# Operand places of the 256-column products, both softmax shares of a head together, and one conditioning half behind the recurrent mixer

## Chip, cores and metric

The kernel runs on one core of one Trainium2 chip. The metric is the device time of one execution in microseconds (us). Every time below is of that one core. The engines are TensorE (PE in the profile, its weight loads PEld), VectorE (DVE), ScalarE (ACT), GpSimd (POOL) and SyncE (SP), which issues most of the DMAs.

## The reference, cut to what matters

A block of two layers over 512 tokens of width 1024, all in fp32. Layer 0 has a gated recurrent mixer (HGRN2), layer 1 a dilated attention of three groups; each is followed by a SwiGLU feed-forward network (FFN). Shift, scale and gate of each half layer come from a conditioning vector `c`.

```python
cond = jax.nn.silu(c)
for layer in range(DEPTH):                                   # 2
    mod = (cond @ ada_w[layer] + ada_b[layer])[:, None, :]   # [1024] x [1024, 6144]
    sh1, sc1, g1, sh2, sc2, g2 = jnp.split(mod, 6, axis=-1)
    u = rms_norm(h, norm_g[layer, 0]) * (1.0 + sc1) + sh1
    y = hgrn2_mixer(u, ...) if layer == 0 else dilated_attention_mixer(u, ...)
    h = h + (1.0 + g1) * rms_norm(y, norm_g[layer, 1])
    u = rms_norm(h, norm_g[layer, 2]) * (1.0 + sc2) + sh2
    gate, up = jnp.split(u @ ffn_w_in, 2, axis=-1)           # [512,1024] x [1024,5632]
    y = (jax.nn.silu(gate) * up) @ ffn_w_out
    h = h + (1.0 + g2) * rms_norm(y, norm_g[layer, 3])
```

In the attention, each group makes an output and a log-sum-exp per token and head; the outputs are weighted by a softmax over the groups:

```python
wts = jax.nn.softmax(jnp.stack(lses, axis=0), axis=0)
o = jnp.einsum('gbsh,gbshd->bshd', wts, jnp.stack(outs, axis=0))
return o.reshape(B, S, D_MODEL) @ w_out
```

## The kernel before, in words

**Products.** An fp32 operand is split into a high and a low part (`hi`, `lo` of weights; `uh`, `ul` of activations, each held as 128 partitions x 8 blocks x 512 tokens), and a product of a 128-row block is three PE passes: high by high, low by high, high by low (L577 to L579 in the helper for the plain products). Most products stream 512 columns. Some are made on 256-column halves:

- `mixer_out` (L699), the mixer's output projection of either layer, streams the halves of tokens for its last blocks, which lets the norm and residual of one half start sooner (L577 to L579 too, 336 products of 128x256 in all).
- `seven_products` (L882), most filters of the FFN's input projection: a filter is 128 gate and 128 up columns, and its 2 x 2 blocks of weights and of tokens are multiplied by seven block products in place of eight, from sums of weight blocks and of token blocks. A filter is seven calls of `run` (L958), of 4 x 3 = 12 products each, 84 in all, at L964. The sums of tokens (`th`, `tl`) are made once ahead (L864 to L879); those of weights per filter by POOL (L935) and DVE (L939, L943), split by ACT (L927, L951) and DVE (L931, L955). The first filters of each FFN (`PLAIN`: three pairs of 256 columns in layer 0, two in layer 1) are made as plain 512-column products. So FFN 0 has 16 filters by sevens and FFN 1 has 18.
- In the attention, queries and keys of two groups and the values (`products`, L1976, issued at L1982) are made by the same kind of seven products on 256 columns.

**Places.** A split weight goes to one of the buffers `hi` or `lo`, 128 x (2048 + 128) elements; `places(i, first)` (L117) lets it begin at column `first` of that buffer, so the stationary operand's byte address can be shifted. The constants R0 = 16 and V0 = 32 (L36) are the columns for the FFN's and the queries' and keys' parts, and for the values' parts. `mixer_out`'s pieces (`Stream.pieces`, L97) begin at column 0. In `seven_products` the first of the seven runs uses the token block B11. For filter 0 it is read where it lies in `uh` and `ul`; `shift()` (L893 to L897) then copies it to 144 columns further on, and all later filters read that copy:

```python
B11 = [u_of(0, 0), [(uh[:, k, 144:400], ul[:, k, 144:400]) for k in range(4)]]
```

**Order of the work.** All 1 MB weight loads, also those of the conditioning matrix `ada_w`, go through one list `items` (L485 and on) and two raw buffers: SP issues the load of an item when a raw buffer is free, and the items are worked off in the order of the list. A weight item costs ACT one cast (L89) and DVE one subtraction (L90); an `ada` item costs DVE four multiply-adds over 128 x 512 (L390, L392), and after the second of a half POOL's `partition_all_reduce` (L394); a `fin` item turns a finished half into columns with four diagonal sums (L404) and small operations (L408, L410). `hg_o` are the four pieces of the recurrent mixer's output weights, `f0a` the loads of FFN 0's input weights (six plain ones, then the filters of the sevens), `shift` the items of the conditioning vector (1, 4), that is layer 1's scale ahead of its FFN: two halves of two loads and one `fin` each. In the stage where the recurrent mixer ends, DVE, PE and POOL follow the order of the program: POOL's power `orr` (L592) gives the inverse root of the head norm, DVE multiplies by it (`aT`, L1589), PE transposes the result (L1596).

**Softmax of groups.** Per head, group 0 (natural token order, N) has its maximum and sum in `sN`, groups 1 and 2 (dilated order, R) in `sR`; each is sent to DRAM and read back in the other order (`oR`, `oN`; POOL issues these DMAs, L2261 and L2282 to L2290). `shares(own, other)` (L2293) works out one side's share with eight small DVE operations and one exponential on ACT; `merged(hd)` (L2309) calls it for R, scales the R probabilities on ACT (L2314), then for N, and scales those (L2319). A planner with costs orders these tasks among the products.

## Time and profile before

| | us |
|---|---|
| median of 3 runs (lowest, highest) | 1510.85 (1510.26, 1512.8) |
| the profiled execution | 1511.48 |
| its span in the trace | 1509.5 |
| PE busy | 1481.1 (98%) |
| DVE busy | 1108.2 (73%) |
| ACT busy | 799.6 (53%) |
| POOL busy | 200.7 (13%) |
| mean granted clock of PE | 0.995 |

The span leaves out 2 us around the program, which are part of the execution's time. A row of the timeline reads: start, duration, engine, line, operation, output<-inputs, shape, count, and in brackets the idle time of the engine just before with what ended it. A matmul's duration overlaps the next one's, so the pace of products is read from the distance of their starts, or from a window's length divided by its products. A row of the windows reads: bounds, sum of busy time, PE's busy time with the count of its instructions, granted clock (1.00 is full), the DMA engines' share, GB/s. A row of the waits reads: engine, what waited, what it waited for, total us, times, longest.

### The profile page before, as it was taken

The page shows a single profiled execution, that of the slowest core. Times are in us where ns is not written, and L with a number is a line of the kernel's source. Part 1 is how long each engine was busy: PE and PEld are TensorE (multiplying, and loading weights), DVE is VectorE, ACT ScalarE, POOL GpSimd, SP SyncE. Part 2 cuts the span into 40 slices and gives each one's busy share as a digit, 9 for nine tenths or more (in the row PEclk, how much of TensorE's full clock was granted, in tenths as well). Part 3 has the DMA queues.
Part 4 walks back from the last instruction along what each step waited for, and adds up shares of the span by engine and source line. Part 5 has one row for each costly group of instructions (what it writes and reads, how often), then busy time and mean ns, then how long its engine had stood idle before and what let it go on. Part 6 is the DMA issues. An engine that isn't in the chain of part 4 may idle for free. (4 is left out here: it accounts for less than half of the span.)

```text
span 1509.5 us, 25145 instructions
## 1 busy us (share of the span) xinstructions
PE 1481.1 (98%) x9807; PEld 1324.4 (88%) x9807; DVE 1108.2 (73%) x1896; ACT 799.6 (53%) x1482; POOL 200.7 (13%) x174
## 2 busy tenths in 40 slices
PE   8999999899999999999999999999999999999998
PEld 6777888788999997888998989999988899999886
DVE  4577768478688876777798777888776978887533
ACT  4443433273455542357647777557886555555231
POOL 1011211131111111131001010001012211110100
PEclk9999999999999999999999999999999999999999
DMA  9553445215233346634344343344343333334531
GB/s 308 165 185 126 154 154 195 84 57 180 86 112 109 115 136 223 225 110 150 105 134 127 105 110 85 108 138 134 92 154 126 100 97 113 113 112 140 195 112 56
DMA packets 210151, 201.09 MB, mean 133 GB/s; under 512 B 8248, under 2 KB 167920, under 8 KB 209776
## 3 DMA queue, kind: packets, MB, share of 16 engines
q1 hardware_dynamic: 207056, 192.71, 40.8%
q10 hardware_dynamic: 1952, 6.65, 1.2%
q8 instruction: 77, 1.26, 0.4%
q0 software_dynamic: 1024, 0.13, 0.2%
q14 instruction: 42, 0.34, 0.1%
HBM read 192.31 MB, written 5.31 MB: 131 GB/s over the span
## 5 line engine op out<-in xcount | busy, mean ns | idle before, releaser
L89 ACT CAST hi<-raw 128x2048 fp32r<-128x2048 f32 x43 | 82.1, 1910 | 135.8 <-DMA raw<-in_ffn_w_out_dram 69.4
L577 PE MATMUL ps_mm<-uh,hi 128*128 128x512 f32 (+1 forms) x400 | 146.3, 366 | 0.0
L578 PE MATMUL ps_mm<-ul,hi 128*128 128x512 f32 (+1 forms) x400 | 144.3, 361 | 1.0 <-DVE ul L677 1.0
L579 PE MATMUL ps_mm<-uh,lo 128*128 128x512 f32 (+1 forms) x400 | 144.6, 361 | 0.0
L1982 PE MATMUL ps_mm<-apart,hiq 128*128 128x256 f32 (+1 forms) x608 | 142.5, 327 | 0.0
L90 DVE TENSOR_TENSOR lo<-raw,hi 128x2048 fp32r<-128x2048 f32 x43 | 101.0, 2352 | 56.3 <-ACT hi L89 56.3
L1982 PEld LDWEIGHTS ps_mm<-apart,hiq 128*128 128x128 f32 x608 | 99.8, 188 | 8.1
L1982 PE MATMUL ps_mm<-apart,loq 128*128 128x256 f32 (+1 forms) x304 | 97.7, 321 | 0.0
L964 PE MATMUL ps_mm<-th,hiq 128*128 128x256 f32 x340 | 93.9, 276 | 0.0
L964 PE MATMUL ps_mm<-tl,hiq 128*128 128x256 f32 x340 | 93.9, 276 | 0.0
L964 PE MATMUL ps_mm<-th,loq 128*128 128x256 f32 x340 | 93.9, 276 | 0.0
L955 DVE TENSOR_TENSOR loq<-raw,hiq 128x1024 fp32r<-128x1024 f32 x68 | 80.2, 1220 | 18.5 <-ACT hiq L951 18.5
L577 PEld LDWEIGHTS ps_mm<-uh,hi 128*128 128x128 f32 x400 | 75.5, 189 | 19.7 <-issue 8.4
L578 PEld LDWEIGHTS ps_mm<-ul,hi 128*128 128x128 f32 x400 | 75.6, 189 | 12.0 <-DVE ul L677 1.4
L579 PEld LDWEIGHTS ps_mm<-uh,lo 128*128 128x128 f32 x400 | 75.5, 189 | 11.5
L935 POOL TENSOR_TENSOR raw<-raw 128x512 f32<-128x512 f32 x34 | 44.7, 1315 | 302.7 <-DVE spare L931 138.2
L577 PE MATMUL ps_mm<-hi,oh 128*128 128x512 f32 x208 | 82.1, 395 | 0.7 <-ACT hi L89 0.7
L578 PE MATMUL ps_mm<-lo,oh 128*128 128x512 f32 x208 | 81.7, 393 | 0.4 <-DVE lo L90 0.4
L951 ACT CAST hiq<-raw 128x1024 fp32r<-128x1024 f32 x68 | 68.0, 1046 | 18.4 <-DVE raw L939 17.5
L1982 PE MATMUL ps_mm<-uh,hiq 128*128 128x256 f32 x256 | 72.6, 283 | 3.4 <-ACT ps_mm L2071 2.9
L1982 PE MATMUL ps_mm<-uh,loq 128*128 128x256 f32 x256 | 71.7, 280 | 0.1
L1982 PE MATMUL ps_mm<-ul,hiq 128*128 128x256 f32 x256 | 71.6, 280 | 0.0
(486 smaller groups left out, 4659.6 us busy)
## 6 DMA issues: line engine op xcount, KB each, us to landing
raw<-in_ada_w_dram SPq DMA_DIRECT2D x40, 1024.0 KB, 5.2
raw<-in_ffn_w_in_dram SPq DMA_DIRECT2D x136, 256.0 KB, 3.7
raw<-in_ffn_w_out_dram SPq DMA_DIRECT2D x22, 1024.0 KB, 5.1
raw<-in_attn_w_in_dram SPq DMA_DIRECT2D x64, 256.0 KB, 4.7
raw<-in_hgrn_w_in_dram SPq DMA_DIRECT2D x12, 1024.0 KB, 5.3
raw<-in_attn_w_in_dram SPq DMA_DIRECT2D x12, 1024.0 KB, 5.0
raw<-in_ffn_w_in_dram SPq DMA_DIRECT2D x10, 1024.0 KB, 5.2
raw<-in_attn_w_in_dram SPq DMA_DIRECT2D x16, 512.0 KB, 5.2
```

Of the source, the lines that this page charges most:

```text
L89: self.nc.scalar.copy(hi, t)
L90: self.nc.vector.tensor_sub(lo, t, hi.bitcast(F32))
L577: pe.matmul(ps, ah, bh, start=start, stop=False, skip_group_check=part)
L578: pe.matmul(ps, ah, bl, start=False, stop=False, skip_group_check=part)
L579: pe.matmul(ps, al, bh, start=False, stop=stop, skip_group_check=part)
L935: pool.tensor_add(r[:, 2], r[:, 2], r[:, 0])
L951: act.copy(hi, src)
L955: dve.tensor_sub(lo, src, hi.bitcast(F32))
L964: pe.matmul(ps, w[x][:, a], us[kt][y], start=begin and kt + m == 0, stop=kt == 3 and m == 2, skip_group_check=True)
L1982: pe.matmul(dst(), x, y, start=begin and i == 0, stop=i == len(todo) - 1, skip_group_check=True)
```

## The change

Three things are changed.

**Places.** The first two `pieces` calls of `mixer_out` begin at column 16. The queries' and keys' parts take a column per head (`Q0`), the values' parts one per unit (`V0`). `shift()` and the copy are gone: every filter's first run reads B11 in its own place. All 256-column products of `mixer_out` and of the FFN then have a distance of 64 between the stationary and the moving operand's byte address, modulo 512.

```diff
-R0, V0 = 16, 32
+R0, V0, Q0 = 16, (112, 96, 64, 16), (16, 16, 16, 16, 48, 80, 112, 0)
...
-            (hi_a, lo_a), (hi_b, lo_b) = st.pieces(2)
+            (hi_a, lo_a), (hi_b, lo_b) = st.pieces(2, first=R0)
...
-            B11 = [u_of(0, 0), [(uh[:, k, 144:400], ul[:, k, 144:400]) for k in range(4)]]
-
-            def shift():
-
-                for a, b in ((112, 256), (0, 112)):
-                    for copy, t in ((act.copy, uh), (dve.tensor_copy, ul)):
-                        copy(t[:, 0:4, a + 144:b + 144], t[:, 0:4, a:b].bitcast(F32))
+            B11 = u_of(0, 0)
...
-                    run(s.first, R, 0, B11[i > 0], True)
+                    run(s.first, R, 0, B11, True)
...
-                    if i == 0:
-                        shift()
...
-                s_["p1"] = split_place(R0)
+                s_["p1"] = split_place(Q0[hd])
...
-                    ps[0] = split_place(V0)
+                    ps[0] = split_place(V0[i * 2 + hf])
```

**Shares.** One tile `so` (128 x 2 x 2 x 4 x 2: own or other, R or N, token tile, maximum or sum) takes the place of `sN`, `sR`, `oN` and `oR`. `merged` works out both shares in one go: six small DVE operations and one exponential per head instead of sixteen and two. The R probabilities' scaling now comes behind both read-backs.

```diff
+            reads = [so("R"), so("oR"), so("oN")] + [so(n, t) for n in "RN" for t in range(NT)]
+            DVE(0.2, lambda: dve.tensor_tensor(M.t, so.t[:, 0, :, :, 0], so.t[:, 1, :, :, 0], op=OP.max), reads, [M()])
+            DVE(0.2, lambda: dve.tensor_sub(e.t, so.t[:, :, :, :, 0], M.t.unsqueeze(1).broadcast_to((P, 2, 2, NT))), reads + [M()], [e()])
+            ACT(0.22, lambda: act.activation(e.t, e.t, AF.Exp), w=[e()])
+            DVE(0.2, lambda: dve.tensor_mul(z.t, e.t, so.t[:, :, :, :, 1]), reads + [e()], [z()])
+            DVE(0.2, lambda: dve.tensor_add(z.t[:, 0], z.t[:, 0], z.t[:, 1]), w=[z()])
+            DVE(0.22, lambda: dve.reciprocal(z.t[:, 0], z.t[:, 0]), w=[z()])
+            DVE(0.2, lambda: dve.tensor_mul(e.t[:, 0], e.t[:, 0], z.t[:, 0]), [z()], [e()])
```

**Order of items.** The second load of the conditioning vector's half 1 and that half's `fin` move from among `hg_o` into FFN 0's plain loads; half 0's `fin` comes earlier.

```diff
-        items += weave(hg_o, shift[1:4], 0)
+        items += [hg_o[0], *shift[1], hg_o[1], shift[3][0], hg_o[2], *shift[2], hg_o[3]]
...
-        items += weave(f0a[:n0], shift[5:] + gate_loads[:2] + [gate_fins[:1]], 2) + f0a[n0:]
+        items += weave(f0a[:n0], [shift[3][1:], shift[5] + gate_loads[0], gate_loads[1], gate_fins[:1]], 2) + f0a[n0:]
```

SP's loads from the mixer's last output weights to the end of FFN 0's plain loads, in the kernel before:

```order
L69 DMA raw_2210<-in_hgrn_w_out_dram 128x4x512
L69 DMA raw_2387<-in_ada_w_dram 128x4x512
L69 DMA raw_2393<-in_hgrn_w_out_dram 128x4x512
L69 DMA raw_2470<-in_ffn_w_in_dram 128x8x256
L69 DMA raw_2476<-in_ffn_w_in_dram 128x8x256
L69 DMA raw_2698<-in_ffn_w_in_dram 128x8x256
L69 DMA raw_2795<-in_ffn_w_in_dram 128x8x256
L69 DMA raw_2965<-in_ada_w_dram 128x4x512
L69 DMA raw_3121<-in_ffn_w_in_dram 128x8x256
L69 DMA raw_3127<-in_ada_w_dram 128x4x512
L69 DMA raw_3133<-in_ffn_w_in_dram 128x8x256
```

and in the changed one:

```order
L69 DMA raw_2210<-in_ada_w_dram 128x4x512
L69 DMA raw_2397<-in_hgrn_w_out_dram 128x4x512
L69 DMA raw_2463<-in_ffn_w_in_dram 128x8x256
L69 DMA raw_2469<-in_ffn_w_in_dram 128x8x256
L69 DMA raw_2691<-in_ffn_w_in_dram 128x8x256
L69 DMA raw_2788<-in_ada_w_dram 128x4x512
L69 DMA raw_2958<-in_ffn_w_in_dram 128x8x256
L69 DMA raw_3105<-in_ada_w_dram 128x4x512
L69 DMA raw_3111<-in_ffn_w_in_dram 128x8x256
L69 DMA raw_3127<-in_ada_w_dram 128x4x512
L69 DMA raw_3133<-in_ffn_w_in_dram 128x8x256
```

The conditioning load that stood ahead of the mixer's last output weights (raw_2387) now stands between FFN 0's third and fourth plain load (raw_2788); the other conditioning load of half 1 stays with the mixer's, now ahead of the last piece alone. The plain loads and the gate's two loads behind it keep their order.

POOL at the recurrent mixer's end, before (`q` is the last decayed query tile, `shared` the conditioning half's sums, `orr` the powers; ISA rows without operands have none that the order names):

```order
L1538 TENSOR_TENSOR q_2140<-qd_2118,fpre_2124 128x512
L394 ISA
L394 ISA shared<-shared 128x512 x2
L592 ISA
L592 TENSOR_TENSOR orr_2315<-rv_2316,expo 128x4
L592 TENSOR_TENSOR orr_2349<-rv_2350,expo 128x4
```

and after:

```order
L1530 TENSOR_TENSOR q_2140<-qd_2118,fpre_2124 128x512
L394 ISA
L394 ISA shared<-shared 128x512
L592 ISA
L592 TENSOR_TENSOR orr_2315<-rv_2316,expo 128x4
L592 TENSOR_TENSOR orr_2349<-rv_2350,expo 128x4
```

One of the two all-reduces ahead of the powers is gone from here.

DVE at the same place, before (`diag` and `cols` are the diagonal sums of a finished half):

```order
L591 TENSOR_SCALAR rv_2316<-oss_2310 128x4
L1570 SCALAR_TENSOR_TENSOR state_2324<-state_2324,ftot_2126,ps_b_2320 128x128 x2
L404 ISA diag_3107,cols<-shared,ident 128x128
L404 ISA cols 128x1
L404 ISA diag_3109,cols<-shared,ident 128x128
L404 ISA cols 128x1
L404 ISA diag_3111,cols<-shared,ident 128x128
L404 ISA cols 128x1
L1589 TENSOR_TENSOR aT_2309<-ps_b_2301,orr_2315 128x512
L404 ISA diag_3113,cols<-shared,ident 128x128
```

and after:

```order
L90 TENSOR_TENSOR lo_2394<-raw_2204,hi_2393 128x2048
L1597 TENSOR_TENSOR Q_2298<-Q_2298,ps_mm_2273 128x512
L591 TENSOR_SCALAR rv_2316<-oss_2310 128x4
L1562 SCALAR_TENSOR_TENSOR state_2324<-state_2324,ftot_2126,ps_b_2320 128x128 x2
L1581 TENSOR_TENSOR aT_2309<-ps_b_2301,orr_2315 128x512
L1599 TENSOR_TENSOR oT_late_694<-oT_late_694,Q_2237 128x512
L591 TENSOR_SCALAR rv_2350<-oss_2344 128x4
```

The diagonal sums of the conditioning half no longer stand between `rv` and `aT`.

More of the change, by code (lines that the diff above doesn't have):

```diff
@@ L766, in mixer_out @@
             mm(3, range(4))
[L767 removed]
+            (hi_a, lo_a), (hi_b, lo_b) = st.pieces(2, first=R0)
             mm(2, range(4, 6))
@@ L2280, in scores_of @@
                 return
-            oR, oN = slot("oR", 2, [P, NT, 2], ap), slot("oN", 2, [P, NT, 2], ap)
-            POOL(0.6, lambda: pool.dma_start(oR.t, scr[hd, 0].rearrange("(l r) s -> l r s", r=4)), [("scr", hd, 0)], [oR()], late=2.2)
-            DVE(0.2, lambda: dve.tensor_tensor(sR.t[:, :, 0], mR.t[:, 0], mR.t[:, 1], op=OP.max), [mR(i, r) for i in (1, 2) for r in range(NT)], [sR()])
-            DVE(0.2, lambda: dve.tensor_scalar(nR.t, sR.t[:, :, 0], -1.0, None, op0=OP.mult), [sR()], [nR()])
+            POOL(0.6, lambda: pool.dma_start(so.t[:, 1, 0], scr[hd, 0].rearrange("(l r) s -> l r s", r=4)), [("scr", hd, 0)], [so("oR")], late=2.2)
@@ L2285, in scores_of @@
+            DVE(0.2, lambda: dve.tensor_tensor(so.t[:, 0, 0, :, 0], mR.t[:, 0], mR.t[:, 1], op=OP.max), [mR(i, r) for i in (1, 2) for r in range(NT)], [so("R")])
+            DVE(0.2, lambda: dve.tensor_scalar(nR.t, so.t[:, 0, 0, :, 0], -1.0, None, op0=OP.mult), [so("R")], [nR()])
             for r in range(NT):
-                ACT(0.6, lambda r=r: act.activation(PR[:, r], PR[:, r], AF.Exp, bias=nR.t[:, r:r + 1], accum_out=sR.t[:, r, 1:2]),
-                    [nR(), sR()], [("PR", 0, 1, r), ("PR", 0, 2, r), sR(r)])
@@ L2288, in scores_of @@
-            POOL(0.6, lambda: pool.dma_start(scr[hd, 1].rearrange("(l r) s -> l r s", r=4), sR.t), [sR()] + [sR(r) for r in range(NT)],
+                ACT(0.6, lambda r=r: act.activation(PR[:, r], PR[:, r], AF.Exp, bias=nR.t[:, r:r + 1], accum_out=so.t[:, 0, 0, r, 1:2]),
+                    [nR(), so("R")], [("PR", 0, 1, r), ("PR", 0, 2, r), so("R", r)])
+            POOL(0.6, lambda: pool.dma_start(scr[hd, 1].rearrange("(l r) s -> l r s", r=4), so.t[:, 0, 0]), [so("R")] + [so("R", r) for r in range(NT)],
@@ L2309, in merged @@
+            POOL(0.75, lambda: pool.dma_start(so.t[:, 1, 1], scr[hd, 1].rearrange("(t p) s -> p t s", p=P)), [("scr", hd, 1)], [so("oN")], late=2.2)
         def merged(hd):
             st_ = heads[hd]
-            rr_ = [st_["sR"]()] + [st_["sR"](r) for r in range(NT)] + [st_["oR"]()]
-            e = shares(st_["sR"], st_["oR"], rr_)
+            so = st_["so"]
+            reads = [so("R"), so("oR"), so("oN")] + [so(n, t) for n in "RN" for t in range(NT)]
+            M, e, z = slot("wM", 2, [P, 2, NT], ap), slot("wE", 2, [P, 2, 2, NT], ap), slot("wZ", 2, [P, 2, 2, NT], ap)
@@ L2313, in merged @@
+            DVE(0.22, lambda: dve.reciprocal(z.t[:, 0], z.t[:, 0]), w=[z()])
+            DVE(0.2, lambda: dve.tensor_mul(e.t[:, 0], e.t[:, 0], z.t[:, 0]), [z()], [e()])
             for r in range(NT):
[L2314 to L2316 removed]
+                ACT(0.42, lambda r=r: act.activation(st_["PR"][:, r], st_["PR"][:, r], AF.Copy, scale=e.t[:, 0, 0, r:r + 1]),
+                    [e()], [("PR", 0, 1, r), ("PR", 0, 2, r)])
```

51 lines of the change are left out of this document (16 added, 35 removed).

## The prediction

> **What bounds the kernel now.** I read the profile's page first: engine totals, then the chain that ended last, then the idle time before each engine.
>
> ```profile
> span 1509.5 us, 25145 instructions
> PE 1481.1 (98%) x9807; PEld 1324.4 (88%) x9807; DVE 1108.2 (73%) x1896; ACT 799.6 (53%) x1482; POOL 200.7 (13%) x174
> PE ps_a L1596 <- DVE aT L1589: 5.1, 1, 5.1
> PE ps_mm L1982 <- ACT ps_mm L2071: 2.9, 2, 2.1
> PE ps_a L2330 <- DVE sN L2253: 1.8, 1, 1.8
> ```
>
> TensorE (PE) is busy 98% of the span, so two things set the time: the rate at which products follow one another, and the few PE waits (last three rows: total, times, longest). The largest wait, 5.1 us, is at the end of the recurrent mixer. So each part of the change is priced at one of these two places. My sum is made against the profiled execution: 1511.48 us, of which the span is 1509.5; the median of the runs shown is 1510.85, 0.63 lower.
>
> Next, the rate. The view of busy time by window (bounds, sum, PE with its count of matmuls, granted clock, DMA share, GB/s) and single starts of the timeline:
>
> ```profile
> 390.63:400.53 9.90, 9.90 (x86) 1.00 0.01 2
> 419.73:421.15 1.42, 1.42 (x14) 1.00 0.69 207
> 421.15:422.53 1.38, 1.38 (x14) 1.00 0.90 256
> 422.53:429.33 6.80, 6.80 (x62) 1.00 0.21 61
> 724.75:734.64 9.89, 9.89 (x85) 1.00 0.35 108
> 1210.10:1220.00 9.90, 9.90 (x85) 1.00 0.01 2
> 1182.30 0.28 PE L579 MATMUL ps_mm<-uh,lo 128*128 128x256 f32 x1
> 1187.70 0.28 PE L579 MATMUL ps_mm<-uh,lo 128*128 128x256 f32 x1
> ```
>
> A filter of the seven products is seven runs of 12, 84 products of 256 columns; each window's count has one or two more, which overlap its edges. All have clock 1.00, yet three rates stand here: 9.90/84 = 117.8 ns (filter 0 of either FFN, and a stretch of 84 in attention at 724.75); 6.80/60 = 113.3 ns (a later FFN filter, behind its first two runs); and 120.0 ns in mixer_out's half products (45 products from 1182.30 to 1187.70). Setting each stretch beside the byte addresses of its operands, with distance = (stationary minus moving address) modulo 512: 120.0 goes with distance 0, while distance 64 has both 117.8 and 113.3. With B11's shifted copy (144 columns, 576 bytes, on) a later filter's first run is at distance 0 and takes 1.42/12 = 118.3; the next takes 115.0; the other five go at 113.3 until the next filter. Filter 0 lacks the shifted run and stays at 117.8 throughout. I read this as two locked paces at distance 64: a stream that comes straight from 512-column products enters the slow one (all three 84-product rows), and the shifted run kicks it into the fast one.
>
> **1. The shift is removed (FFN).** Every filter of both FFNs then has filter 0's distances, all 64, and enters from the same 512-column products. With no kick and no PE stall inside the stage, I take 9.90 for every filter in place of 1.42+1.38+6.80 = 9.60: with 16 filters in FFN 0 (15 after the first) and 18 in FFN 1 (17), 32 x 0.295 = **+9.4 us** (4.4 and 5.0). The other bound is a stream that is fast from its first product: 84 x 113.3 ns = 9.52, so 32 x -0.08 and twice -0.38: -3.3. I choose the slow end because the entry itself, the one thing that decides, is shown by the filter-0 rows and doesn't change. The four copies of the shift per FFN lay on ACT and DVE beside PE work: nothing.
>
> **2. mixer_out's halves at column 16.** 336 products leave distance 0 for 64: 120.0 to 117.8 or 113.3, so -0.7 to -2.2. They too follow 512-column products: **-0.7**.
>
> **3. Attention's places.** Q0 and V0 also move the query, key and value operands, and the fused softmax tile, 128 bytes larger, moves the other moving operand (apart) by 128 bytes more. Of the new distances (448, 192, 320, 256, 128 and others) only 384, in the value units, has rows here:
>
> ```profile
> 751.00:765.00 14.00, 14.00 (x121) 1.00 0.14 41
> 853.10:857.00 3.90, 3.90 (x37) 1.00 0.04 3
> 815.37:818.08 2.71, 2.71 (x24) 1.00 0.21 47
> ```
>
> Value units now run at about 118.6 ns (14.00 over some 118 products), and query/key products (distance 64) at both paces: 3.90 over some 34.4 (113.5), and 2.71 over 23 (117.8). Against the nearest rows: 672 value products could gain 672 x 5.3 ns = 3.6 or lose 672 x 1.4 = 0.9; of the 1344 query/key products some three in four stand at the slow pace by the timeline (mean 116.7), and could gain 1344 x 3.2 = 4.3 or lose 1344 x 3.3 = 4.4 (to 120.0). That is -8 to +5.3. Few of the new distances are 0, so I take **-1**.
>
> [...]
>
> **4. The conditioning half behind the mixer.** The mixer's end, on POOL, DVE and PE:
>
> ```profile
> 250.39 3.25 POOL L394 PARTITION_ALL_REDUCE shared<-shared  x1 [13.07 <-DVE shared L392]
> 271.73 3.23 POOL L394 PARTITION_ALL_REDUCE shared<-shared  x1 [18.09 <-DVE rv L591]
> 282.73 1.05 POOL L592 TENSOR_TENSOR orr<-rv,expo 128x4 f32<-128x4 f32 x1 [7.77 <-issue]
> 271.47 0.16 DVE L591 TENSOR_SCALAR rv<-oss 128x4 f32<-128x4 f32 x1
> 283.81 0.69 DVE L1589 TENSOR_TENSOR aT<-ps_b,orr 128x512 f32<-128x512 f32 x1 [7.85 <-POOL orr L592]
> 284.65 1.09 PE L1596 MATMUL ps_a<-ident,aT 128*128 128x128 f32 x4 [5.08 <-DVE aT L1589]
> 284.65:288.53 3.88, 3.88 (x12) 0.50 0.00 0
> ```
>
> The power (orr) needs rv, ready at 271.6, but stands behind the second all-reduce (to 274.96) and a further 7.77 us with no instruction that the profile shows. DVE waits for it, and PE for DVE, 5.08 us; the last row shows PE at half clock for 3.88 us afterwards, 1.94 lost. By the order, only half 0's all-reduce (250.39) now stands before the power; the same 7.77 behind it ends near 262, before rv. aT could then be made near 273, ahead of PE's need at 279.5. That removes 5.08 + 1.94 = **-7.0**. What is late next is the second rv, aT pair and the last w_out piece; PE has other products from 284.65 to 291.26 between, so I leave up to 3 us of it: -4 to -7.
>
> The work lands in FFN 0's plain stage. Its loads, the casts, and PE's need:
>
> ```profile
> 332.84 0.37 SPq L69 DMA_DIRECT2D raw<-in_ffn_w_in_dram  x1
> 339.29 0.37 SPq L69 DMA_DIRECT2D raw<-in_ada_w_dram  x1
> 347.17 0.37 SPq L69 DMA_DIRECT2D raw<-in_ffn_w_in_dram  x1
> 354.16 0.37 SPq L69 DMA_DIRECT2D raw<-in_ada_w_dram  x1
> 358.63 0.37 SPq L69 DMA_DIRECT2D raw<-in_ffn_w_in_dram  x1
> raw<-in_ada_w_dram SPq DMA_DIRECT2D x40, 1024.0 KB, 5.2
> 365.76 2.28 DVE L90 TENSOR_TENSOR lo<-raw,hi 128x2048 fp32r<-128x2048 f32 x1
> 365.98 5.17 POOL L394 PARTITION_ALL_REDUCE shared<-shared  x1 [29.53 <-DVE shared L392]
> 379.75 0.39 PE L577 MATMUL ps_mm<-uh,hi 128*128 128x512 f32 x1
> 381.77 2.36 DVE L955 TENSOR_TENSOR loq<-raw,hiq 128x1024 fp32r<-128x1024 f32 x2 [0.39 <-ACT hiq L951]
> 392.05 0.28 PE L964 MATMUL ps_a<-th,hiq 128*128 128x256 f32 x1
> ```
>
> Two raw buffers serve this stream, and SP issues in order, so one more 1 MB load (its DMA, four DVE chunks, an all-reduce and four diagonal sums) pushes every later one by a step: 4.5 to 8 us between these issues, 11.5 if the chunks also wait behind DVE's sums. The last w_in piece, lo from 365.76 to 368.04, is needed at 379.75 (48 plain products of 226.7 ns before 390.63): 11.7 us of slack. Filter 0's sums (loq from 381.77 to 384.13), needed at 392.05, have 7.9. A push of 8 costs nothing; one of 11.5 costs 3.6 there. The nearest measured cover is short, so I take **+3.5**, bounds 0 and +8 (a push of 14, and the clock lost as after the mixer's wait).
>
> [...]
>
> **5. Softmax shares.** Per head ten small DVE operations and one ACT exponential go; each takes some 0.16 us, 8 x 10 x 0.16 = 13 us of DVE.
>
> ```profile
> 895.62 0.15 DVE L2302 TENSOR_TENSOR wZ<-wE,sR 128x4 f32<-128x4 f32 x1
> 892.17 0.75 POOL L2290 DMA_DIRECT2D oN<-scr  x1 [1.52 <-DMA scr<-sR]
> ```
>
> DVE is 73% busy beside PE, so little of that reaches the end: at most a share of the 1.8 us wait on L2253. Against it, the group-R scale now also waits for oN, issued by POOL at 892.17, where this head's share arithmetic went on at 895.62; behind the waiting DVE operation stand casts and score drains that PE reads. That costs nothing if oN lands by then, and up to 2 us at some heads otherwise. **-0.5**, bounds -1.5 and +3.
>
> **Sum:** -7.0 + 3.5 + 9.4 - 0.7 - 1 - 0.5 = +3.7: 1511.5 + 3.7 - 0.6 = **1514.6 us**, slower by 0.25%. With terms 2 to 5 all at their low or all at their high ends 1502 and 1532; half of that each way, as they are independent: 1508 to 1523.
>
> **Rivals.**
> - FFN 0 enters fast and FFN 1 slow. If the plain stage's late loads stall PE at filter 0, the pace is drawn anew: the query/key stretch of 853.10 (113.5 ns) began behind fp32 scores, while that of 815.37, just behind the 2.1 us wait on L2071, stayed slow. FFN 0 then gives -1.6 instead of +4.4: 1514.6 - 6 = 1508.6. Against it: a stall must fall behind the first 256-column product.
> - Faster: both FFNs run fast without the kick, because the pace depends on something else that changes (mixer_out's halves, no longer at 120.0, end ahead of them). Decided at the first product of each FFN's filter 0; worth -1.6 - 1.7 instead of +9.4: 1501.9. Against it: FFN 0 and 1 entered at the same slow pace though they came from mixers of different kinds, and 724.75 too.
> - Places do nothing, the later filters being faster for another reason (their operands are prepared while PE runs): terms 1 to 3 go: 1511.5 - 4 - 0.6 = 1506.9. [...] The step from 117.8 to 113.3 just behind the shifted run speaks against it.
> - The mixer's wait stays, since an all-reduce and the idle behind it still stand before the power, or returns as a longer one in the plain stage: +7 on the sum: 1521.6. For it: POOL's rows still hold that pair; against it, 250.39 leaves 17 us.
>
> **Chances.** Forecast 0.53, FFN 0 fast 0.22, both fast 0.11, no effect of places 0.05, wait kept or moved 0.09. About 0.2% (3 us, below 1507.8 or above 1513.9) is what a measurement of this kernel can tell from no change. Forecast: 0.56 slower, 0.38 same, 0.06 faster; FFN 0 fast: 0.4 faster, 0.5 same; both fast and, by half, no effect: faster; the last: slower. So faster 0.26, same 0.34, slower 0.40. The range reaches down to the second rival's time and up to the forecast's own upper end, which takes in the last rival's: 1502 to 1523.
>
> **What would show it.** Right: filters of 9.90 us everywhere in both FFNs, no wait on aT near 280 and clock 1.00 there, a PE wait of a few us at 376 to 395 less the time saved. Wrong: later filters at 9.5 to 9.6 (term 1), mixer_out's halves still at 120.0 (term 2), attention's value units beyond 113.3 to 120.0 ns (term 3), a wait on aT (term 4), new PE waits on the shares (term 5).

## The result

The changed kernel takes 1515.4 us (median of 10 runs, 1512.63 to 1520.53) against 1510.84 for the kernel before (10 runs beside it, 1507.8 to 1515.21): a ratio of 1.003, with a 95% interval of 1.0016 to 1.0044. It is slower, by about as much as the 1514.6 us that was forecast. But that the sum came out so close is partly luck: two large misses, the shares and FFN 0's pace, point in opposite directions, as the experiments show.

### The profile after

Totals, and the longest waits of PE and DVE (the latter in the attention, 705 to 1170 us) in the changed kernel:

```profile
span 1516.1 us, 25045 instructions
PE 1487.4 (98%) x9807; PEld 1329.4 (88%) x9807; DVE 1100.0 (73%) x1812; ACT 797.3 (53%) x1470; POOL 199.9 (13%) x174
PE ps_mm L1974 <- DVE loq L2046: 2.9, 2, 2.1
PE ps_a L2313 <- ACT h L2298: 2.4, 1, 2.4
PE ps_a L958 <- ACT hiq L945: 1.4, 1, 1.4
DVE wM L2290 <- DMA so<-scr: 12.7, 7, 5.1
```

DVE lost 84 operations (80 of the shares, four copies of B11), and yet PE is busy 6.3 us longer: its products follow one another more slowly, at the slow pace or at half clock. Waits are not counted as busy. The wait of 5.1 us on aT is gone from the list. In its place stand waits in the attention, one at FFN 0's entry (L958 <- L945), and on DVE a new one: the shares' first operation stands 12.7 us in all, 5.1 once, for the read-back from DRAM.

The pace of the FFNs' products (windows of one filter each):

```profile
385.63:389.17 3.54, 3.54 (x19) 0.52 0.68 191
389.17:398.69 9.52, 9.52 (x86) 1.00 0.52 148
398.69:408.21 9.52, 9.52 (x86) 1.00 0.30 85
1221.89:1231.78 9.89, 9.89 (x86) 1.00 0.33 97
```

FFN 1 (last row) takes 9.89 us per filter throughout, the slow pace that filter 0 had before. FFN 0 runs at 9.52 in this execution: it entered slowly, met two waits in its second run, went at half clock for some 3.5 us (first row), and came out fast.

The recurrent mixer's end, on POOL, DVE and PE:

```profile
250.08 3.25 POOL L394 PARTITION_ALL_REDUCE shared<-shared  x1 [14.79 <-DVE shared L392]
270.12 1.06 POOL L592 TENSOR_TENSOR orr<-rv,expo 128x4 f32<-128x4 f32 x1 [16.79 <-DVE rv L591]
271.22 0.69 DVE L1581 TENSOR_TENSOR aT<-ps_b,orr 128x512 f32<-128x512 f32 x1 [0.62 <-POOL orr L592]
```

The power follows rv at once, and aT is ready at 271.9. The all-reduce is still there ahead of the power. If the 7.77 us behind it are too, both are over by some 261 us, well before rv.

And FFN 0's entry, on PE:

```profile
384.15 0.38 PE L958 MATMUL ps_a<-th,hiq 128*128 128x256 f32 x1 [1.35 <-ACT hiq L945]
385.41 0.39 PE L958 MATMUL ps_a<-th,loq 128*128 128x256 f32 x1 [0.76 <-DVE loq L949]
```

Stage by stage, from the starts of the first products of each (profiled executions, us):

| stage | before | after | difference |
|---|---|---|---|
| start to mixer_out's half products, layer 0 | 319.55 | 310.40 | -9.15 |
| to FFN 0's sevens | 69.89 | 69.63 | -0.26 |
| FFN 0's sevens | 153.79 | 156.55 | +2.76 |
| FFN 0's output | 169.44 | 169.57 | +0.13 |
| attention | 447.92 | 457.04 | +9.12 |
| mixer_out of layer 1 | 37.30 | 36.56 | -0.74 |
| FFN 1's plain products and sevens | 183.93 | 188.90 | +4.97 |

(The first row begins at PE's first product, the rows of sevens at the stage's first 256-column product. The rows sum to +6.8; the spans differ by 6.6.) Of the first row, 2.0 is there at 25 us already (the kernel before was at half clock for 6.8 us from 15.46, the changed one was not); from the 1590th product (268.74 us before) to the 1800th, the mixer's end itself, it is -7.1. Of the attention's +9.12, 5.1 lie at its last head: from group 0's send to DRAM to mixer_out it takes 52.97 us instead of 47.83. Two further stretches of 3.4 us at half clock, at 890.85 and 972.77, cost some 1.7 each; the profile before has none in the attention.

### The profile page after: what moved, and what is told of

Its sections match the earlier page's. It is cut to its first block, busy times and chain, and to the rows that moved or that the text cites. A ratio compares the mean times of both kernels' runs of the same rounds, so it can differ in the third digit from the quotient of the medians.

```text
span 1516.1 us, 25045 instructions
## 1 busy us (share of the span) xinstructions
PE 1487.4 (98%) x9807; PEld 1329.4 (88%) x9807; DVE 1100.0 (73%) x1812; ACT 797.3 (53%) x1470; POOL 199.9 (13%) x174
## 5 line engine op out<-in xcount | busy, mean ns | idle before, releaser
L958 PE MATMUL ps_mm<-th,hiq 128*128 128x256 f32 x340 | 95.2, 280 | 0.0
L958 PE MATMUL ps_mm<-tl,hiq 128*128 128x256 f32 x340 | 95.1, 280 | 0.0
L958 PE MATMUL ps_mm<-th,loq 128*128 128x256 f32 x340 | 95.0, 279 | 0.0
L578 PEld LDWEIGHTS ps_mm<-ul,hi 128*128 128x128 f32 x400 | 75.3, 188 | 12.2 <-DVE ul L677 1.5
L945 ACT CAST hiq<-raw 128x1024 fp32r<-128x1024 f32 x68 | 68.1, 1047 | 17.3 <-DVE raw L933 15.6
```

What stands on the lines that cost most here:

```text
L578: pe.matmul(ps, ah, bl, start=False, stop=False, skip_group_check=part)
L945: act.copy(hi, src)
L958: pe.matmul(ps, w[x][:, a], us[kt][y], start=begin and kt + m == 0, stop=kt == 3 and m == 2, skip_group_check=True)
```

## The experiments

The theory: each FFN's products have two paces that hold until something disturbs the stream, the shifted copy of B11 set the fast one, and its loss costs most; the mixer's wait is gained. Rivals: places do nothing; the attention's loss comes from places; or it comes from the shares. All ratios are to the kernel before, run beside.

### One part at a time

**The shift alone.** B11 is read where it lies; nothing else changes.

```diff
-            B11 = [u_of(0, 0), [(uh[:, k, 144:400], ul[:, k, 144:400]) for k in range(4)]]
+            B11 = u_of(0, 0)
...
-                    if i == 0:
-                        shift()
```

> The kernel before with one thing changed: B11's shifted copy is gone, every filter's first run reads B11 where it lies. Theory of the two locked paces: nothing in either FFN moves the products off the slow pace, all 34 filters take 9.90 us instead of 9.60 (filter 0 as now), +9.4 us, about 1520; the trace shows 117.8 ns throughout both FFNs. Rival, the pace belongs to the places alone (all runs at distance 64 like the last five of a filter now, 113.3 ns): about -3, 1508. Rival, the later filters are faster for another reason than the shift: 1511 and 113.3 ns.

Measured: 1521.72 us, ratio 1.0069 (1.0057 to 1.0081), all five runs within 1521.63 to 1523.45. A filter of FFN 0 and one of FFN 1:

```profile
420.00:429.90 9.90, 9.90 (x87) 1.00 0.39 106
1235.18:1245.08 9.90, 9.90 (x87) 1.00 0.37 107
```

All filters take 9.89 us at clock 1.00 with no wait in either stage: 32 x 0.29 = 9.3 of the 10.4 us that the ratio gives (8.6 to 12.2). Both rivals, that places do nothing and that distance 64 is fast by itself, fall.

**The order of items alone.**

```diff
-        items += weave(hg_o, shift[1:4], 0)
+        items += [hg_o[0], *shift[1], hg_o[1], shift[3][0], hg_o[2], *shift[2], hg_o[3]]
...
-        items += weave(f0a[:n0], shift[5:] + gate_loads[:2] + [gate_fins[:1]], 2) + f0a[n0:]
+        items += weave(f0a[:n0], [shift[3][1:], shift[5] + gate_loads[0], gate_loads[1], gate_fins[:1]], 2) + f0a[n0:]
```

> The kernel before with the order of items of the changed one and nothing else. Theory: the wait of 5.1 us on aT and the 1.9 us lost at half clock behind it go (-7, at most -9), FFN 0's plain stage gives some of it back through late loads (0 to +4 at the entry of filter 0): about 1504 to 1507. Since the shifted run is there, the pace of both FFNs from filter 1 on is 113.3 ns whatever the entry. Rival, the moved work costs as much in FFN 0 as it cost in the mixer: 1510 to 1512.

Measured: 1507.51, ratio 0.9966 (0.9955 to 0.9977). The wait on aT is gone, FFN 0's sevens take 155.20 instead of 153.79 (+1.4, with a gap of 1.0 us between two starts in filter 0), and from filter 1 on every filter takes 9.60, as the theory has it. -7.1 + 1.4 = -5.7, against a measured -0.34%, 5.1 us. The row of aT, PE's wait in FFN 0's filter 0, and three runs behind it:

```profile
269.67 0.69 DVE L1589 TENSOR_TENSOR aT<-ps_b,orr 128x512 f32<-128x512 f32 x1 [0.62 <-POOL orr L592]
384.27 0.38 PE L964 MATMUL ps_a<-th,loq 128*128 128x256 f32 x1 [0.75 <-DVE loq L955]
385.53:389.61 4.08, 4.08 (x39) 1.00 0.86 247
```

These three runs already go at 4.08/36 = 113.3 ns, behind a wait and before any shifted run. So it is FFN 1 that shows here what the shifted run does (filter 0 at 117.8, later ones at 9.60 us); in FFN 0 the stream was fast before it.

**The shares alone.** `so` and the fused `merged` of the changed kernel, with `pad` at 64 columns, so that the attention's operands stay where they were.

```diff
-        up.tile([P, 96], F32, name="pad")
+        up.tile([P, 64], F32, name="pad")
```

> The kernel before with both softmax shares of a head made together, and nothing else (the space ahead of the attention's operands is cut by 128 bytes, so that these keep their places). Theory on record: -0.5 us (-1.5 to +3), ten small DVE operations per head fewer against a later scaling of the R probabilities. Rival, seen in the changed kernel's trace: DVE stands 2 to 2.5 us at the shares' first operation at two heads, waiting for the read-back, and PE behind it: +3 to +6.

Measured: 1517.4, ratio 1.0033 (1.002 to 1.0047). This is the term that was wrong. DVE, POOL and PE at the last head in this kernel:

```profile
1121.94 0.56 POOL L2287 DMA_DIRECT2D scr<-so  x1
1125.64 0.77 POOL L2289 DMA_DIRECT2D so<-scr  x1 [3.14 <-DMA scr<-so]
1128.59 0.17 DVE L2298 TENSOR_TENSOR wM<-so 128x8 f32<-128x8 f32 x1 [5.04 <-DMA so<-scr]
1131.01 2.30 PE L2321 MATMUL ps_a<-ident,h 128*128 128x128 f32 x8 [2.41 <-ACT h L2306]
1131.00:1134.80 3.80, 3.17 (x11) 0.70 0.49 122
1134.80:1142.00 7.20, 7.20 (x34) 0.69 0.50 177
```

and the same head in the kernel before:

```profile
1120.10 0.17 DVE L2298 TENSOR_TENSOR wM<-sR,oR 128x4 f32<-128x4 f32 x1 [0.96 <-DMA oR<-scr]
1125.08 0.16 DVE L2298 TENSOR_TENSOR wM<-sN,oN 128x4 f32<-128x4 f32 x1 [1.32 <-DMA oN<-scr]
```

Before, the R share starts at 1120.10, and its scaling and PE's transposes of R run while oN is on its way. Together, both wait for the second of two round trips through DRAM, issued in series by POOL: DVE stands 5.04 us at the head of its queue, PE waits 2.41 us, and the mean clock in the next 11 us is 0.7 (last two rows). That loses 0.30 x 3.80 + 0.31 x 7.20 = 3.4 us more; with the wait 5.8, against a measured 5.0.

**The attention's places alone.** Q0, V0, and `pad` at 128 columns, so that the moving copy `apart` lies 128 bytes on, as in the changed kernel.

```diff
-R0, V0 = 16, 32
+R0, V0, Q0 = 16, (112, 96, 64, 16), (16, 16, 16, 16, 48, 80, 112, 0)
...
-        up.tile([P, 96], F32, name="pad")
+        up.tile([P, 128], F32, name="pad")
```

> The kernel before with the attention's operands at the changed kernel's places (Q0, V0, and the moving copy 128 bytes further on), and nothing else. Theory on record: -1 us (-8 to +5.3), the query, key and value products' paces move between 113.3 and 120.0 ns. From the changed kernel's trace, values at 113 to 120 instead of 118.6 and queries and keys with more of the slow pace: -2 to +2. Rival, what the changed kernel lost between 724 and 1165 us (some 9 us in its profiled execution) is a matter of places: +5 to +9.

Measured: 1513.76, ratio 1.0012 (1.0003 to 1.0021). The rival is out, but the sign of the term on record (-1) was wrong too. The groups of 512-column products on `apart` (busy, mean ns of one), in this kernel:

```profile
L1982 PE MATMUL ps_mm<-apart,hiq 128*128 128x512 f32 x224 | 71.5, 400 | 0.0
L1982 PE MATMUL ps_mm<-apart,loq 128*128 128x512 f32 x112 | 44.2, 395 | 0.0
```

In the kernel before these two read 70.7, 397 and 43.9, 392. Every product's duration is some 3 ns longer, and by their starts they follow at some 232.5 ns in place of 228.5, which is 384 x 4 = 1.5 us. The forecast had counted the 256-column products only. Those did become a little faster: waits left out, they follow one another at 116.8 ns on average in this profile, and at 117.1 to 117.4 in three profiles with the old places (`before`, `shift_gone`, `shares_alone`), which for 2016 products is some 0.5 to 1 us.

### What it is about the shares

**The wait without the fusion.** The kernel before with its separate shares, but oN is added to the reads that the planner is given for R's first operation.

```diff
-            rr_ = [st_["sR"]()] + [st_["sR"](r) for r in range(NT)] + [st_["oR"]()]
+            rr_ = [st_["sR"]()] + [st_["sR"](r) for r in range(NT)] + [st_["oR"](), st_["oN"]()]
```

> The kernel before, its two shares separate as they are (sixteen small DVE operations per head), but the R share's first operation also waits for oN, as in the changed kernel. Theory: what the shares made together cost (about 5 us) is this wait, a POOL queue with two DMA round trips in series at whose end DVE stands, worst at the last head: 1515 to 1518, with a DVE wait of 3 to 5 us at the last head near 1124 us. Rival, the cost comes from the wider operations or the planner's other order: within 1 us of before.

Measured: 1513.49, ratio 1.0015 (1.0005 to 1.0024), between the theory's 1515 to 1518 and the rival's 1510.4 to 1512.4. The edit did not do what was expected of it: it binds the planner alone. At the last head R's first operation still runs behind oR, before oN has landed. But the planner now puts N's first operation ahead of the rest of R's, so that the rest (L2302) stands behind oN all the same, and with it oT, for which PE waits 5.0 us:

```profile
1121.25 0.16 DVE L2298 TENSOR_TENSOR wM<-sR,oR 128x4 f32<-128x4 f32 x1 [0.72 <-DMA oR<-scr]
1125.19 0.16 DVE L2298 TENSOR_TENSOR wM<-sN,oN 128x4 f32<-128x4 f32 x1 [3.51 <-DMA oN<-scr]
1125.47 0.16 DVE L2302 TENSOR_TENSOR wZ<-wE,sR 128x4 f32<-128x4 f32 x1
PE ps_mm L579 <- DVE oT L2426: 5.0, 1, 5.0
```

What the last head costs can be read from the time between POOL's send of group 0 (L2261) and mixer_out's first half product in layer 1, in the profiled executions:

| kernel | send at (us) | to mixer_out (us) |
|---|---|---|
| before | 1113.96 | 47.83 |
| `shares_alone` | 1116.46 | 53.47 |
| `wait_only` | 1108.79 | 55.37 |
| `last_head_apart` (next) | 1113.99 | 48.96 |

So R's share standing behind oN costs as much there without the fusion (7.5 us) as with it (5.6). The total of `wait_only` is smaller because its execution had gained some 5 us in the attention ahead of that send, where the planner's order is another; where that gain comes from was not followed up.

**All heads fused but the last.** For head 7 the six operations run twice, on the R half of `so` as soon as oR is there, then on the N half.

```diff
+            parts = [slice(0, 1), slice(1, 2)] if hd == 7 else [slice(0, 2)]
+            for n, k in enumerate(parts):
+                w = k.stop - k.start
+                if w == 1:
+                    reads = [so("RN"[n]), so(("oR", "oN")[n])] + [so("RN"[n], t) for t in range(NT)]
...
-            DVE(0.2, lambda: dve.tensor_tensor(M.t, so.t[:, 0, :, :, 0], so.t[:, 1, :, :, 0], op=OP.max), reads, [M()])
+                DVE(0.2, lambda k=k: dve.tensor_tensor(M.t[:, k], so.t[:, 0, k, :, 0], so.t[:, 1, k, :, 0], op=OP.max), reads, [M(n)])
```

> Both shares made together for heads 0 to 6, for the last head one after the other (R as soon as oR is there), the attention's operands at the places of before. Theory: the cost of the shares sits at the last head, where no product is left to cover it, and most of the 5 us goes: 1510 to 1512.5. Rival, every head pays a part: 1514 to 1516. In either case the wait of 5 us on DVE near 1124 us is gone.

Measured: 1511.25, ratio 1.0 (0.9989 to 1.0012). The whole cost goes with the last head's wait:

```profile
1120.49 0.16 DVE L2303 TENSOR_TENSOR wM<-so 128x4 f32<-128x4 f32 x1 [1.63 <-DMA so<-scr]
1125.40 0.16 DVE L2303 TENSOR_TENSOR wM<-so 128x4 f32<-128x4 f32 x1 [1.41 <-DMA so<-scr]
```

The fusion of heads 0 to 6 costs nothing that these runs can tell, and saves nothing either.

### What sets the pace

**One shifted run per FFN.** Only filter 1 reads the shifted copy; B11 is then copied back.

```diff
+            def unshift():
+
+                for a, b in ((0, 112), (112, 256)):
+                    for copy, t in ((act.copy, uh), (dve.tensor_copy, ul)):
+                        copy(t[:, 0:4, a:b], t[:, 0:4, a + 144:b + 144].bitcast(F32))
...
-                    run(s.first, R, 0, B11[i > 0], True)
+                    run(s.first, R, 0, B11[i == 1], True)
...
-                    if i == 0:
-                        shift()
+                    if i < 2:
+                        (shift, unshift)[i]()
```

> The kernel before, but only filter 1 of each FFN reads the shifted copy of B11; behind its first run B11 is copied back, and filters 2 and on read it where it lies, as in the changed kernel. Theory of locked paces: one run at distance 0 sets the fast pace for the whole stage: filters 2 and on take 9.52 us instead of 9.60, 30 x -0.08 = -2.4, about 1508.5. Rival, each filter needs its own shifted run: they fall back to 9.90, +9 us, as with no shift at all. The copying back lies beside products: nothing.

Measured: 1520.43, ratio 1.0062 (1.0044 to 1.0081): by the number, the rival. The trace tells more. The windows are filter 1's five runs behind the first two, and a later filter; then the moment between, on PE and ACT:

```profile
400.56:407.27 6.71, 6.71 (x62) 1.00 0.46 131
408.90:418.79 9.89, 9.89 (x86) 1.00 0.37 108
407.26 0.28 PE L970 MATMUL ps_mm<-th,loq 128*128 128x256 f32 x1
407.38 0.39 PE L970 MATMUL ps_mm<-uh,hiq 128*128 128x256 f32 x1
407.61 0.28 PE L970 MATMUL ps_mm<-ul,hiq 128*128 128x256 f32 x1
403.76 1.28 ACT L903 CAST uh<-uh 128x448 fp32r<-128x448 f32 x2
406.97 0.36 ACT L1021 COPY shared<-ps_mm 128x256 f32<-128x256 f32 x1
```

The run made the stream fast. Then the product of 407.38, the first of PE's seventh run, is followed only after 0.23 us, twice the usual. The trace names no wait there. But the drain (L1021) ends at 407.33, only 0.05 us ahead of that run, and in the kernel before 0.8 us ahead of it (417.59 and 418.38): ACT is late behind the 1.28 us of copying back. From that product on the pace is slow, in both FFNs. So a hesitation of 0.1 us went with the loss of the pace; that it is the cause is argued, not shown.

**The mixed version, first try.** The same kernel with the changed order of items and mixer_out's pieces at column 16 (`st.pieces(2, first=R0)`).

```diff
-        items += weave(hg_o, shift[1:4], 0)
+        items += [hg_o[0], *shift[1], hg_o[1], shift[3][0], hg_o[2], *shift[2], hg_o[3]]
...
-            (hi_a, lo_a), (hi_b, lo_b) = st.pieces(2)
+            (hi_a, lo_a), (hi_b, lo_b) = st.pieces(2, first=R0)
...
-                    run(s.first, R, 0, B11[i > 0], True)
+                    run(s.first, R, 0, B11[i == 1], True)
```

> The kernel before with the changed order of items (-4 to -5), mixer_out's first pieces at column 16 (-1 by the changed kernel's trace: 0.3 and 0.7 in the two stages), and one shifted run per FFN (-2.4); shares, attention's places and the other runs as before. Theory, the terms add up: about -8, 1502 to 1504. Rival, the late loads that FFN 0's entry shows grow into the gain: 1506 to 1508.

Measured: 1510.09, ratio 0.9994 (0.9979 to 1.0009), 1503.09 to 1516.25: neither theory nor rival, and the widest spread of all. In the profiled execution FFN 0 ran at 9.52 us per filter and FFN 1 at 9.89: FFN 1 lost its pace as above, while FFN 0, fast since a wait of 0.8 us in its filter 0, met a like hesitation (400.7 us) and stayed fast. So such a hesitation doesn't always lose the pace.

**Distance 0 without the copy.** The changed kernel, with filter 1's R weights at column 0 instead of 16, so that its runs on R are at distance 0.

```diff
+    def part_views(self, firsts):
+        self.count = getattr(self, "count", 0) + 1
+        ts = [self.pool.tile([P, 2048 + 128], F32R, name=f"{tag}q{self.count}", tag=tag, bufs=self.parts) for tag in ("hi", "lo")]
+        return [[t[:, f:f + 2048] for t in ts] for f in firsts]
...
-                    ring.append((spare if p == 0 else st.part_tiles(R0), st.part_tiles(R0)))
-                return ring[p]
+                    ring.append(((spare,) if p == 0 else tuple(st.part_views((R0, 0)))) + (st.part_tiles(R0),))
+                return ring[p][i == 1], ring[p][-1]
```

> The changed kernel, but in filter 1 of each FFN the R weights lie at column 0 instead of 16, so that four of its seven runs are at distance 0; nothing is copied, all other filters are as in the changed kernel. Theory of locked paces, in which a wait of 0.1 us behind the copying back was what undid the single shifted run: the fast pace is set in filter 1 and stays, FFN 1's filters take 9.52 us instead of 9.89 (16 x 0.37 = -5.9), FFN 0's too wherever it would have been slow: 1508 to 1510.5. Rival, a pace doesn't last beyond its filter: 1515, as the changed kernel.

Measured: 1521.59, ratio 1.0063 (1.0046 to 1.008). Filter 1's first run in FFN 1, and a filter behind it:

```profile
1227.38:1228.82 1.44, 1.44 (x14) 1.00 1.03 300
1237.35:1247.25 9.90, 9.90 (x87) 1.00 0.38 108
```

1.44/12 = 120.0 ns, a third pace, and the slow one behind it. (Three of the filter's seven runs use R and go at 120.0; the expectation's four is a miscount.) So distance 0 alone is not what sets the fast pace, and the reading that it does is refuted. In the shifted run both operands begin 64 bytes past a multiple of 128; here both begin at a multiple of 128, as in mixer_out's half products, which run at 120.0 too. In FFN 0 the runs on R did the reverse. Four runs of filter 0, behind the waits of its entry, and filter 2:

```profile
389.65:395.09 5.44, 5.44 (x50) 1.00 0.20 56
405.06:414.95 9.89, 9.89 (x86) 1.00 0.36 107
```

Filter 0 had come out fast, 5.44/48 = 113.3 ns, as in the changed kernel's profiled execution; from the first run on R the stream is slow. The slowest and fastest of the six runs lie only 2.9 us apart, and all six are slower than the slowest of the changed kernel's ten (1520.53). The two kernels differ by 0.33%, 5.0 us, where FFN 0 at 9.52 in place of 9.89 is worth 15 x 0.37 = 5.6. That speaks for FFN 0 having been fast in most of those ten runs.

**The pace held to the end, and the mixed version again.** As `best`, but filters 1 and 2 read the shifted copy, and the copying back goes in two pieces, one per filter, so that ACT is held up half as long at a time.

```diff
-                    run(s.first, R, 0, B11[i > 0], True)
+                    run(s.first, R, 0, B11[i in (1, 2)], True)
...
                     if i == 0:
                         shift()
+                    elif i < 3:
+                        unshift(*((0, 112), (112, 256))[i - 1])
```

> The kernel before with the changed order of items, mixer_out's first pieces at column 16, and the shifted copy of B11 read by filters 1 and 2 of each FFN alone; it is copied back in two pieces, one per filter, so that ACT is held up half as long each time and PE's seventh run no longer waits 0.1 us. Theory of locked paces: the fast pace set by the shifted run now stays to the end of each FFN, 9.52 us per filter from filter 3 on, 117.8 ns nowhere behind filter 0: order -4 to -5, mixer_out -1, FFNs 29 x -0.08 = -2.3, about 1503 to 1505. Rival, the pace falls back by itself a filter or two behind the last shifted run: 1511 to 1514.

Measured: 1504.88 (1500.69 to 1505.64), ratio 0.9941 (0.9925 to 0.9958): the fastest of all. In FFN 1, a filter soon behind the last shifted run, and the last filter:

```profile
1243.87:1253.39 9.52, 9.52 (x87) 1.00 0.38 110
1367.63:1377.03 9.40, 9.40 (x85) 1.00 0.65 225
```

From filter 3 on all filters take 9.52 in both FFNs (the last 9.40 up to its last start). Two shifted runs set the pace for the 15 filters behind them, 1260 products. The rival falls. With the copying in two pieces the drain ends 0.5 to 0.6 us ahead of the seventh run, and no hesitation is seen. FFN 0 also shows that a wait doesn't always make a stream fast: behind waits of 1.55 and 0.8 us at its entry, four runs of filter 0 still go at 5.65/48 = 117.7 ns, and only the shifted run ends that.

```profile
389.97:395.62 5.65, 5.65 (x50) 1.00 0.19 56
```

### Two more

**512-column products back at distance 0.** `attn_places` with the first group's weights at column 32.

```diff
-                s_["p"] = p = plan.place("hl", 3, lambda: st.part_tiles(0))
+                s_["p"] = p = plan.place("hl", 3, lambda: st.part_tiles(32))
```

> The kernel before with the attention's operands at the changed kernel's places, and the 512-column weights of the first group moved by 32 columns (128 bytes), as the moving copy has moved. Theory: of the cost of the attention's places (+1.8 us) 384 x 5.5 ns = 2.1 comes from the 512-column products, whose distance went from 0 to 384 with the moving copy; back at 0 they take 227 ns again: 1510 to 1512 (-2 against the kernel with the places alone). Rival, the cost is in the 256-column products' paces: 1513 to 1514.

Measured: 1512.79, ratio 1.0002 (0.9991 to 1.0013). The two groups read

```profile
L1982 PE MATMUL ps_mm<-apart,hiq 128*128 128x512 f32 x224 | 70.7, 397 | 0.0
L1982 PE MATMUL ps_mm<-apart,loq 128*128 128x512 f32 x112 | 43.8, 391 | 0.0
```

as in the kernel before, to 1 ns; by their starts they follow at 228.8 ns. The pace of these products went with the distance of their two operands: moving one by 128 bytes changed it (397 to 400 ns and 392 to 395), moving the other too restored it. That the 1.8 us of `attn_places` is theirs alone is not shown: the two intervals overlap, and in the profiled executions the attention takes 449.8 and 450.4 us, hardly more than in kernels whose attention is unchanged (447.5 to 449.7).

**The conditioning half moved further.** No shifted copy, filter 1's R weights at column 0, mixer_out's pieces at column 16, and all of half 1 among FFN 0's output weights.

```diff
-        items += weave(hg_o, shift[1:4], 0)
+        items += [hg_o[0], *shift[1], hg_o[1], shift[3][0], *hg_o[2:]]
...
-        items += weave(f0b, gate + [gate_fins[1:] + rest[0]] + rest[1:], 0, 0.8)
+        items += weave(f0b, gate + [gate_fins[1:] + shift[2], shift[3][1:], shift[5] + rest[0]] + rest[1:], 0, 0.8)
```

> The kernel before without the shifted copy; filter 1's R weights at column 0 as in after_kick; mixer_out's first pieces at column 16; and all of the conditioning vector's half 1 (two loads and its sums) behind FFN 0's filters, among the loads of its output weights, instead of at the mixer's end. Shares and attention's places as before. Theory: the mixer's wait goes (-9 as with the changed order), no late loads at FFN 0's entry (which cost 1.4 to 2.8 there), FFNs at 9.52 from filter 2 on (-2.4), mixer_out -1: 1499 to 1502. Rival, FFN 0's output stage, whose loads already wait for one another, pays for the moved half what the mixer saves: 1505 to 1508.

Measured: 1516.55, ratio 1.0027 (1.0013 to 1.004). Both parts missed. The FFNs stay slow (9.89, for the reason that `after_kick` shows), and FFN 0's output stage grows from 169.4 to 174.6 us:

```profile
643.32 0.51 PE L582 MATMUL ps_mm<-hi,oh 128*128 128x512 f32 x1 [1.36 <-ACT hi L89]
646.01 0.79 PE L583 MATMUL ps_mm<-lo,oh 128*128 128x512 f32 x1 [2.19 <-DVE lo L90]
```

FFN 0's entry has no wait here (filter 0 takes 9.89), so the late loads there do come from the moved half; but the output stage, whose loads already wait for one another, pays 5 us for it: the two waits shown, 3.6 us, and the rest behind them, where the products of 646.01 and 646.60 last 0.79 and 0.63 us in place of 0.39.

## Why the prediction was right, and where it was not

- **The shift (forecast +9.4, measured +10.4 alone).** The sizing held: filter 0's pace is what all filters take without the copy, and the rival by which places do nothing is out. What does not hold is distance 0 as the kick: `after_kick` has it and no fast pace. What the runs show is a pace that lasts (1344 products slow in `shift_gone`, 1260 fast in `best3`), that the shifted run makes fast and runs at 120.0 ns make slow, and that a wait can win or lose. In the changed kernel the term failed in one half: only FFN 1 ran slow in the profiled execution, FFN 0 went fast at the waits of its entry. Here the prediction stood against itself: this term assumed no PE stall inside the stage, while the +3.5 of the moved loads was such a stall in filter 0. It had the outcome as a rival. How often it happens among the ten runs can't be read from their times alone, but by `after_kick` it is in most of them.
- **mixer_out (-0.7, measured -0.75 and -0.73 in the half products themselves, -1.5 in all).** Right in sign, and twice the size: the forecast took 117.8 ns for all of them, and most run at 113.3, some at 117.8. (In layer 0's row of the table only -0.26 is left, since the plain products behind the halves take 0.5 us longer; why is open.)
- **Attention's places (-1, measured +1.8).** Wrong in sign. What the sum counted, the 256-column products, did gain some 0.5 to 1 us. But the moving copy's 128 bytes also moved 384 products of 512 columns from distance 0 to 384, which the sum had put at nothing: +1.5. The remaining 1 us or so is within the interval (0.5 to 3.2).
- **The conditioning half (-7.0 and +3.5, measured -7.1 and +1.4 alone).** The gain is right in place and size, the half clock behind the wait included. The late loads made PE wait in filter 0 as worked out, for less than half of what was taken, when alone; in the changed kernel's profiled execution it was two waits, 1.6 and 1.0 us from start to start, with half a clock behind them, and filter 0 took 13.86 us instead of 9.89.
- **The shares (-0.5, measured +5.0).** The worst term. The prediction saw that R would wait for oN and priced it at up to 2 us at some heads, from a head with products to cover it (L2290 at 892.17). At the last head nothing covers it, and 3.4 us of half clock came on top of the wait, which the sum had not counted here.

The measured parts alone sum to +10.4 - 5.1 + 5.0 + 1.8 - 1.5 = +10.6, where the whole change is +4.6. Of the difference of 6.0, FFN 0's pace accounts for up to 5.6, where the late loads win it back. The forecast's +3.7 left that out as a rival, and the shares' +5.0 by mistake; that these two misses nearly cancel is luck. Of the prediction's own signs of being wrong two appeared: later filters at 9.52 us in FFN 0, and PE waits on the shares.

## What to carry to other kernels

Where one engine is busy 98% of the time, look at the pace of its instructions, not only at its waits: start-to-start times of equal products showed 113.3, 117.8 and 120.0 ns, and 4% of a stage lay in which of them it had fallen into. When several results are to be worked out in one go, ask which of their inputs comes last and what covers that wait at the end of the loop; where there is no cover, leave that turn apart. (Fusing the covered turns gained nothing here that could be told.) A transfer moved out of a full stage was paid for in the next one where that one had too little slack (1.4 us in `order_alone`, 5 us in `best2`); read the slack from the due times of its operands before moving it.

## What the runs showed of the hardware

- The same instruction (256 columns, clock 1.00) follows itself at 113.3, 117.8 or 120.0 ns; the first two at the very same addresses, lasting for over a thousand products. What state holds the pace, and why a run on operands 64 bytes past a multiple of 128 sets the fast one, stays open.
- A disturbance can change the pace either way, and its length doesn't decide. Hesitations of 0.1 us between two products were followed by the slow pace (9.89 us per filter) in both FFNs of `kick_once` (407.38) and in FFN 1 of `best`, not in FFN 0 of `best`. At FFN 0's entry waits were followed by the fast pace in the changed kernel (1.35 and 0.76 us), `order_alone` (0.75), `best` (0.8) and `after_kick` (113.3 ns from 389.65 on), not in `best3` (1.55 and 0.8 us, then 117.7 ns).
- 512-column products have more than one pace too: about 228.5 ns with their operands at distance 0 (the kernel before), and 232.5 at 384 (`attn_places`).
- A wait of 5.1 us in the kernel before went with half clock (0.50 from 284.65 to 288.53) and one of 2.4 us with a lowered clock (0.70 over the 11 us behind it, in `shares_alone`), while one of 2.1 us in the kernel before did not (815.37, clock 1.00). In the profiles of the kernel before and of the changed one, all changes to and from half clock lie on one grid of 3.41 us (in the changed one 385.68, 389.09, 890.85, 894.27, 972.77, 976.19, 1126.37, 1133.20 and 1512.08 us), and what goes with them is how busy PE was in the last stretch of that grid. Two stretches ahead of half clock in the changed kernel, and the two into which the 2.1 us wait of the kernel before falls:

```profile
382.27:385.68 3.41, 1.30 (x9) 1.00 0.00 0
969.36:972.77 3.41, 1.39 (x12) 1.00 0.00 0
810.77:814.18 3.41, 2.23 (x20) 1.00 0.55 132
814.18:817.59 3.41, 2.44 (x20) 1.00 0.07 10
```

  PE was busy 1.3 and 1.4 us ahead of half clock, and 2.2 and 2.4 us where the wait fell across two stretches and the clock stayed. In these two profiles, from 20 us on, the seven stretches at full clock in which PE was busy for 1.4 us or less (0.00 to 1.39) were each followed by half clock, and none of the others (2.17 or more) was. Why the clock goes with it is not shown.
